# A hybrid decoder layer on one core: the first four weight chunks loaded and split by pairs of k tiles, norm1's gains in a DMA of their own, two DMAs on ScalarE's queue

## The chip, the core and the metric

The kernel runs on one core of a Trainium2 chip. The time is that of one execution on the device, in microseconds. The kernel before took 441.95 us (median of 3 runs, 441.61 to 442.01).

## What is computed

One layer of a decoder trunk with two token mixers side by side and a gated feed-forward network, for 256 tokens of width 1024 in float32:

```python
h = rmsnorm(x, norm1_g)
u = h @ w_in                         # 1024 -> 7168: rnn_x, rnn_gate, q, k, v, two branch gates
A = gelu(rnn_gate) * rg_lru(causal_dwconv4(rnn_x))
B = attention(q, k, v)               # 8 heads of 128, causal, q and k normalised
y = sigmoid(g_A) * (A @ w_proj_rnn) + sigmoid(g_B) * (B @ w_proj_attn)
x = x + y @ w_out
h = rmsnorm(x, norm2_g)
x = x + (gelu(causal_dwconv3(h @ w_up)) * (h @ w_gate)) @ w_down
```

## The kernel before

**Products in three parts.** Every weight and every activation is split into two numbers of TensorE's fast float32 form: `hi` (a rounding copy of `raw`) and `lo` (`raw - hi`). A product is three matmuls, `hi*hi`, `hi*lo` and `lo*hi` (`mm3`, L301 to L304). So for each chunk of weights there is one copy, mostly on ScalarE (L284), one subtraction on VectorE (L285), and 24 or 48 matmuls on TensorE.

**Chunks.** The weights stream through the core in 75 chunks of 1 MB (128 partitions by 2048 numbers; a few are smaller), in the order of `UNITS` (L35) and of the feed-forward part. SyncE's queue loads them, up to three ahead of the one being split (`advance`, L287; `AHEAD_L`). Three buffers hold `raw`, four `hi`, three `lo`. `AFTER` (L37) is a table written out by hand: after such a quarter of such a unit's matmuls, these splits (`s5` is the split of chunk 5) and these other steps stand next in program order. The order within each engine is settled from it when the kernel is built.

**The start.** The first unit, `rx`, is the projection to `rnn_x`: four chunks (0 to 3, 256 columns each, the columns of one chunk at one k tile of 128 rows being 256 numbers of a partition) for eight k tiles. The tiles of x transposed, `xT`, are scaled by norm1's gains into `xgh` (ScalarE, L382) and `xgl` (VectorE, L385); the gains are eight columns of the parameter table `vec` (128 by 170), which is one DMA, `pv` (L324), on ScalarE's queue. All four chunks come in pieces, `pieces` (L333): k tile 0, k tile 1, then k tiles 2-3, 4-5, 6-7; each piece of each chunk has a DMA of its own, 128 KB for one k tile and 256 KB for two (L343 to L347). For the first two pieces, those of chunks 2 and 3 are issued on ScalarE's queue, four DMAs, between which stands the loading of an activation table (L349). The DMAs share eight completion semaphores, and the second two of these four wait on ScalarE's queue until the DMA before them on their semaphore has landed. The split of the pieces (L378 to L387) follows the same order, k tile by k tile; the very first copy is on VectorE. TensorE multiplies nine blocks of ones first (L328 to L330, `warm`), and then takes k tile after k tile, for each the four chunks (`run_unit`, L660 to L667): per chunk and k tile two column halves of three matmuls, six of 128x256, and 192 in all.

**What comes next.** The token sums of norm1 (`norm1_stats`, L393) need `xs`, x by rows, which is loaded between the pieces of k tiles 4-5 and 6-7. They are sent to all partitions by two matmuls with ones (`norm1_bcast`, L402, `rbcp`), copied to `rbc`, and scale the results (`rx_evac`, L437). Then come the `rg` chunks (4 to 7), and the rest of the layer.

## Time and profile before

| | |
|---|---|
| median of 3 runs | 441.95 us (441.61 to 442.01) |
| the profiled execution | 442.97 us, its span 441.2 us |
| TensorE (PE) busy | 435.9 us, 99% of the span |
| VectorE (DVE), ScalarE (ACT) busy | 323.9 us, 260.6 us |
| moved by DMA | 91.68 MB |

The profile is of one execution. PE is TensorE's matmuls, PEld its weight loads, DVE VectorE, ACT ScalarE, SPq and ACTq the queues on which SyncE and ScalarE issue DMAs. Times in the views are microseconds from the span's start; the rows of a timeline are merged where like instructions follow each other (`x3`), the second column is then the length of all of them together, and what stands in brackets is the idle time before and what ended it. The span's start and end leave 1.8 us of the execution's time outside.

### The profile page before, as it was taken

What the parts mean: (1) busy time and instruction counts of PE and PEld (TensorE: products, weight loads), DVE (VectorE), ACT (ScalarE), POOL (GpSimd) and SP (SyncE); (2) the same over time, 40 slices, a digit from 0 to 9 for tenths busy, and PEclk for the clock granted to TensorE, in tenths of its full rate; (3) what the DMA queues carried; (4) which work ended last, traced back from release to release, by engine and by line L of the source; (5) the groups of instructions that cost most, each with busy time, mean ns of one, the idle gap of its engine ahead of it and who ended that gap; (6) DMA issues with size and microseconds to landing.
All of it is one profiled execution on the core that took longest, in us unless ns stands there. A gap on an engine that the chain in (4) does not pass through costs nothing.

```text
span 441.2 us, 5822 instructions
## 1 busy us (share of the span) xinstructions
PE 435.9 (99%) x2256; PEld 373.2 (85%) x2256; DVE 323.9 (73%) x477; ACT 260.6 (59%) x309; POOL 1.6 (0%) x9
## 2 busy tenths in 40 slices
PE   8999999999999999999999999999999999999996
PEld 8999988887888888888888888888878888888985
DVE  3688995979999775754576796468789775788463
ACT  4686875999996989752322384315737554455420
POOL 1000000000000000000000000000000000000000
PEclk9999999999999999999999999999999999999999
DMA  7996536453584653454553554989579598289302
GB/s 209 386 345 236 191 111 249 173 209 102 187 255 123 192 193 114 171 192 179 194 190 104 192 190 133 318 230 326 174 260 348 193 343 345 90 309 351 110 0 95
DMA packets 27387, 91.68 MB, mean 208 GB/s; under 512 B 2528, under 2 KB 10080, under 8 KB 23264
## 3 DMA queue, kind: packets, MB, share of 16 engines
q1 hardware_dynamic: 26640, 90.71, 60.3%
q10 hardware_dynamic: 720, 0.61, 0.6%
q8 instruction: 17, 0.28, 0.2%
q14 instruction: 10, 0.08, 0.1%
HBM read 85.02 MB, written 6.29 MB: 207 GB/s over the span
## 4 chain that ended last, share of the span: by engine, by line
PE 93%; ACT 5%; DMA 1%; issue 0%; DVE 0%; SPq 0%; ACTq 0%
PE acc L303 4%; PE acc L304 4%; PE acc L302 4%; PE up L304 4%; PE up L302 4%; PE gt L302 4%; PE gt L304 4%; PE gt L303 4%; PE up L303 4%; PE rx L302 2%; PE rx L303 2%; PE rx L304 2%; PE rg L303 2%; PE rg L302 2%; PE rg L304 2%; PE gb L302 2%
## 5 line engine op out<-in xcount | busy, mean ns | idle before, releaser
L285 DVE TENSOR_TENSOR lo<-raw,hi 128x2048 fp32r<-128x2048 f32 (+3 forms) x92 | 170.6, 1866 | 29.6 <-issue 11.4
L284 ACT CAST hi<-raw 128x2048 fp32r<-128x2048 f32 (+3 forms) x88 | 137.5, 1577 | 66.6 <-PE pa L304 16.1
L303 PE MATMUL acc<-lo,fah 128*128 128x512 f32 x80 | 31.2, 391 | 0.0
L303 PE MATMUL gt<-lo,h2h 128*128 128x512 f32 x80 | 31.2, 390 | 0.0
L303 PE MATMUL up<-lo,h2h 128*128 128x512 f32 x80 | 31.2, 390 | 0.0
L304 PE MATMUL up<-hi,h2l 128*128 128x512 f32 x80 | 31.1, 389 | 0.0
L304 PE MATMUL acc<-hi,fal 128*128 128x512 f32 x80 | 31.1, 389 | 0.0
L302 PE MATMUL up<-hi,h2h 128*128 128x512 f32 x80 | 31.1, 390 | 0.0
L304 PE MATMUL gt<-hi,h2l 128*128 128x512 f32 x80 | 31.0, 389 | 0.0
L302 PE MATMUL acc<-hi,fah 128*128 128x512 f32 x80 | 30.6, 389 | 0.0
L302 PE MATMUL gt<-hi,h2h 128*128 128x512 f32 x80 | 30.5, 389 | 0.0
L302 PE MATMUL rx<-xgh,hi 128*128 128x256 f32 x64 | 18.9, 298 | 0.7 <-ACT xgh L382 0.7
L303 PE MATMUL rx<-xgl,hi 128*128 128x256 f32 x64 | 18.8, 293 | 0.0
L304 PE MATMUL rx<-xgh,lo 128*128 128x256 f32 x64 | 18.8, 293 | 0.0
L829 ACT ACTIVATE fc<-fu,pv 128x256 f32<-128x256 f32 x20 | 10.4, 592 | 13.7 <-DVE fu L841 13.7
L302 PE MATMUL rg<-xgh,hi 128*128 128x256 f32 x64 | 18.2, 284 | 0.0
L303 PE MATMUL rg<-xgl,hi 128*128 128x256 f32 x64 | 18.1, 283 | 0.0
L304 PE MATMUL rg<-xgh,lo 128*128 128x256 f32 x64 | 18.1, 283 | 0.0
L303 PEld LDWEIGHTS acc<-lo,fah 128*128 128x128 f32 x80 | 15.0, 188 | 3.5 <-DVE lo L285 0.5
L302 PEld LDWEIGHTS gt<-hi,h2h 128*128 128x128 f32 x80 | 15.0, 188 | 3.2
L304 PEld LDWEIGHTS up<-hi,h2l 128*128 128x128 f32 x80 | 15.0, 188 | 3.1
L304 PEld LDWEIGHTS acc<-hi,fal 128*128 128x128 f32 x80 | 15.0, 188 | 3.1
(247 smaller groups left out, 1061.3 us busy)
## 6 DMA issues: line engine op xcount, KB each, us to landing
raw<-in_win_tm SPq DMA_DIRECT2D x12, 1024.0 KB, 4.8
raw<-in_win_fm SPq DMA_DIRECT2D x11, 1024.0 KB, 5.7
raw<-in_wup SPq DMA_DIRECT2D x11, 1024.0 KB, 6.0
raw<-in_wgate SPq DMA_DIRECT2D x11, 1024.0 KB, 6.5
raw<-in_wdown SPq DMA_DIRECT2D x11, 1024.0 KB, 6.4
raw<-in_wpr SPq DMA_DIRECT2D x4, 1024.0 KB, 4.9
raw<-in_wpa SPq DMA_DIRECT2D x4, 1024.0 KB, 4.9
raw<-in_wout SPq DMA_DIRECT2D x4, 1024.0 KB, 4.8
```

Source lines behind the costliest of these rows:

```text
L284: (nc.vector.tensor_copy if on_dve else nc.scalar.copy)(hi[i][:, s], raw[i][:, s])
L285: nc.vector.tensor_sub(lo[i][:, s], raw[i][:, s], f(hi[i][:, s]))
L302: nc.tensor.matmul(o, ah, bh, start=start, stop=False, skip_group_check=skip)
L303: nc.tensor.matmul(o, ah, bl, start=False, stop=False, skip_group_check=skip)
L304: nc.tensor.matmul(o, al, bh, start=False, stop=stop, skip_group_check=skip)
L829: nc.scalar.activation(c, u, AF.Identity, scale=w(2), bias=pv[:, V_FB + m:V_FB + m + 1])
```

## The change

Three edits at the start, and a table of order to go with them.

- **Gains first.** `g1`, a tile of 128 by 8, gets norm1's columns of `vec` in a DMA of its own, the first on ScalarE's queue (32 bytes of each partition). The whole table `pv` is loaded later, on SyncE's queue behind the chunks' pieces.
- **Pieces.** The four chunks are loaded by pairs of k tiles (a = 0 to 3) and pairs of chunks (c = 0, 1), eight pieces of 512 KB; a piece is a tile of 128 by 1024, `sraw`, with rows of 2 KB. The first, (0, 0), is two DMAs of 256 KB: chunk 0 on ScalarE's queue, chunk 1 on SyncE's. Everything else is on SyncE's queue, so that ScalarE issues two DMAs, `g1` and this one. `xs` comes behind all pieces.
- **Splits and products.** The first piece is split in quarters (chunk, k tile) of 128x256, the other seven each in one copy and one subtraction of 128x1024. TensorE takes pairs of k tiles, for each the four chunks: twelve matmuls of one chunk on end, 24 of a piece.
- **Order.** `AFTER` is written anew for the whole layer; two edges (`issue_after`) keep what stands after `rx0` behind the last split of the start.

The core of the diff, with the table of order cut to a few lines:

```diff
-    "rg0.1": "bcast",
-    "rg0.2": "s5 evac1",
-    "rg0.3": "s6",
-    "rg1.1": "evac0",
-    "rg1.3": "evac3 conv0 s7",
+    "rg0.2": "bcast evac1",
+    "rg1.1": "s5 evac0",
+    "rg1.2": "conv0 conv1",
...
-    pv = const.tile([P, V_N], F32, name="pv")
-    nc.scalar.dma_start(pv, vec)
+    g1 = const.tile([P, KT], F32, name="g1")
+    nc.scalar.dma_start(g1, vec[:, V_G1:V_G1 + KT])
...
+    def load_x(a, b):
         nc.sync.dma_start(kt(xTs.half(a // 4))[:, a % 4:a % 4 + b - a, :], xT[:, a:b, :])
-        for i in range(START):
-            s = slice(a * 256, b * 256)
-            (nc.scalar if b <= 2 and i >= 2 else nc.sync).dma_start(raw[i][:, s], stream[i][:, s])
-        if a == 0:
-            nc.scalar.preload_act_table(AF.Exp)
-        if a == 4:
-            for t in range(2):
-                nc.sync.dma_start(xs[:, t, :], x[t * P:(t + 1) * P, :])
+
+    def load_w(q, a, c, js=slice(0, 2)):
+        q.dma_start(sraw[a, c][:, js].rearrange("p c k n -> p c (k n)"),
+                    win_fm[2 * c + js.start:2 * c + js.stop, :, a * 512:(a + 1) * 512].rearrange("c p n -> p c n"))
+
+    load_x(0, 1)
+    load_w(nc.scalar, 0, 0, slice(0, 1))
+    nc.scalar.preload_act_table(AF.Exp)
+    load_w(nc.sync, 0, 0, slice(1, 2))
+    load_x(1, 2)
+    load_w(nc.sync, 0, 1)
+    for a in range(1, 4):
+        load_x(2 * a, 2 * a + 2)
+        for c in range(2):
+            load_w(nc.sync, a, c)
+    pv = const.tile([P, V_N], F32, name="pv")
+    nc.sync.dma_start(pv, vec)
+    for t in range(2):
+        nc.sync.dma_start(xs[:, t, :], x[t * P:(t + 1) * P, :])
...
+        def split_x(k):
+            g = g1[:, k:k + 1]
+            nc.scalar.activation(xgh[k], xTs[k], AF.Copy, scale=g)
+            return lambda: nc.vector.scalar_tensor_tensor(xgl[k], xTs[k], g, f(xgh[k]), op0=OP.mult, op1=OP.subtract)
+
+        def split_w(a, c, js=slice(0, 2), ks=slice(0, 2), e=nc.scalar.copy):
+            r, h, l = sraw[a, c][:, js, ks], shi[a, c][:, js, ks], slo[a, c][:, js, ks]
+            start_end[0] = e(h, r).ins
+            return lambda: start_end.__setitem__(1, nc.vector.tensor_sub(l, r, f(h)).ins)
+
+        one, two_ = slice(0, 1), slice(1, 2)
+        x0 = split_x(0)
+        w0 = split_w(0, 0, one, one, nc.vector.tensor_copy)
+        x0()
+        w0()
+        w1 = split_w(0, 0, two_, one)
+        w1()
+        w0 = split_w(0, 0, one, two_)
+        x1 = split_x(1)
+        x1()
+        w0()
+        split_w(0, 0, two_, two_)()
+        split_w(0, 1)()
+        for a in range(1, 4):
+            for k in (2 * a, 2 * a + 1):
+                split_x(k)()
+            for c in range(2):
+                split_w(a, c)()
...
-            for k in range(KT):
+            for a in range(KT // 2):
                 for n in range(START):
-                    fm_mm(rx_ps[n], n, xgh, xgl, (k,), True)
+                    fm_mm(rx_ps[n], n, xgh, xgl, (2 * a, 2 * a + 1), True)
```

More of the change, by code (lines that the diff above doesn't have):

```diff
@@ L1 @@
-from contextlib import ExitStack
+from contextlib import ExitStack, nullcontext
 import concourse.bass as bass
@@ L38 @@
     "rx0.0": "stats s4",
-    "rg0.1": "bcast",
-    "rg0.2": "s5 evac1",
-    "rg0.3": "s6",
-    "rg1.1": "evac0",
-    "rg1.3": "evac3 conv0 s7",
+    "rg0.2": "bcast evac1",
+    "rg1.1": "s5 evac0",
+    "rg1.2": "conv0 conv1",
     "rg2.0": "evac2",
-    "rg2.1": "decay conv1",
+    "rg2.1": "decay",
+    "rg2.2": "s6",
+    "rg2.3": "s7",
     "rg3.0": "split0",
     "rg3.1": "s8",
+    "rg3.2": "evac3",
     "k0.0": "s9",
@@ L50 @@
     "k0.2": "conv3",
-    "k0.3": "split1",
     "k1.0": "s10",
-    "k1.3": "s11",
+    "k1.2": "s11",
     "k2.1": "s12",
-    "k2.2": "s13",
-    "k3.1": "s14 gelu1",
-    "ri0.2": "krs",
-    "ri0.3": "s15",
+    "k2.2": "split1 s13",
+    "k3.2": "gelu1",
+    "k3.3": "s14",
+    "ri0.1": "s15",
     "q0.1": "la0 s16 lb0",
     "q1.1": "s17",
-    "q1.3": "lc0",
-    "ri1.0": "s18",
-    "q2.0": "ld0",
-    "q2.1": "s19",
-    "q2.2": "la1",
-    "q3.0": "lb1 Tq0",
+    "q1.2": "krs",
+    "q2.2": "s18 la1",
+    "q2.3": "s19 lc0",
+    "q3.0": "Tq0",
     "q3.1": "ks0",
     "q3.2": "gelu0",
+    "q3.3": "lb1",
     "v0.1": "qrs",
     "v0.3": "s20 Tk0",
-    "v1.1": "s21",
+    "v1.2": "ld0",
+    "v1.3": "s21",
     "v2.1": "S0 s22",
-    "v3.0": "ks1",
-    "v3.1": "Tk1",
-    "v3.2": "s23",
+    "v2.3": "ks1",
+    "v3.2": "s23 Tk1",
     "v3.3": "lc1 S1 S2",
-    "ga0.2": "s24 P0",
+    "ga0.0": "P0",
+    "ga0.2": "s24",
     "ga1.0": "S3",
-    "ga1.1": "s25 P1 O0",
+    "ga1.1": "s25",
+    "ga1.2": "P1 Tq1",
     "ga1.3": "s26",
-    "ga2.0": "Tq1",
-    "ga2.1": "P2",
+    "ga2.0": "P2",
+    "ga2.1": "O0",
     "ga2.3": "s27",
-    "ga3.1": "P3",
-    "ga3.2": "O1 S5 S6",
-    "ga3.3": "S7 O3",
-    "gb0.1": "S4",
-    "gb0.3": "s28",
-    "gb1.0": "O2",
-    "gb1.2": "ld1 s29",
-    "gb1.3": "P4",
-    "gb2.0": "s30 s31",
-    "gb2.1": "P6 ya0 ya1 O4",
-    "gb2.3": "P5",
-    "gb3.0": "P7",
-    "gb3.1": "ys0",
+    "ga3.0": "P3",
+    "ga3.1": "S5",
+    "ga3.2": "O1 S6",
+    "ga3.3": "O3",
+    "gb0.0": "O2 S4",
+    "gb0.2": "S7 s28",
+    "gb1.0": "ld1",
+    "gb1.3": "s29 P4",
+    "gb2.0": "ya1 s30",
+    "gb2.1": "P6 s31 O4",
+    "gb2.2": "s32",
+    "gb2.3": "P5 P7",
+    "gb3.1": "sb0 ya0 ys0",
     "gb3.3": "ys1",
-    "pr0.0": "s32 sb0",
+    "pr0.0": "s33",
     "pr0.2": "sa0",
-    "pr0.3": "s33",
-    "pr1.0": "O7",
+    "pr0.3": "O7",
     "pr1.2": "s34",
-    "pr2.0": "sa1 O6",
-    "pr2.2": "O5",
+    "pr2.0": "sa1",
+    "pr3.2": "O5",
     "pr3.3": "sb1",
-    "pa0.0": "s35 s36",
+    "pa0.0": "s35 O6 s36",
     "pa0.3": "s37",
@@ L109 @@
     "pa2.1": "s39",
-    "pa2.2": "s40 m0",
+    "pa2.2": "m0",
     "pa3.3": "m1",
-    "wo.3": "s41",
-    "wo.4": "m2",
-    "wo.6": "m3",
+    "wo.0": "s40",
+    "wo.6": "m2",
+    "wo.7": "s41 m3",
     "wo.11": "n10 s42",
     "wo.12": "n00",
-    "wo.14": "s43",
+    "wo.13": "s43",
     "up00.0": "n01 s44",
-    "up00.1": "n11",
+    "up00.1": "n11 s45",
     "up00.3": "bcast2",
-    "gt00.0": "s45",
     "up01.0": "s46",
-    "gt01.0": "s47",
-    "gt01.1": "ur0",
-    "up10.1": "s48",
-    "up10.2": "gr0",
-    "up11.1": "s49",
-    "up11.3": "fu0",
+    "gt01.1": "s47",
+    "gt01.3": "ur0",
+    "up10.2": "s48 s49",
+    "up11.2": "gr0",
     "gt10.1": "s50",
-    "gt10.2": "ur1",
+    "gt10.2": "fu0 ur1",
     "gt11.1": "s51 fg0",
     "up20.1": "s52",
-    "up20.2": "gr1",
-    "up20.3": "fu1",
+    "up20.2": "fu1",
+    "up21.0": "gr1",
     "up21.1": "s53",
     "gt20.1": "s54",
-    "gt20.2": "ur2",
-    "gt20.3": "fg1",
-    "gt21.1": "s55",
+    "gt21.0": "ur2 fg1 s55",
     "dn0.1": "s56",
     "dn0.2": "gr2",
-    "dn0.3": "fu2",
     "dn1.1": "s57",
     "up30.1": "s58",
-    "up30.3": "fg2",
-    "up31.1": "s59",
-    "gt30.1": "s60",
-    "gt30.2": "ur3",
-    "gt31.1": "s61",
-    "dn2.1": "s62",
+    "up30.2": "fu2",
+    "up31.3": "s59",
+    "gt30.1": "fg2 s60 s61",
+    "gt31.1": "s62",
+    "dn2.0": "ur3",
     "dn2.2": "gr3",
@@ L153 @@
     "dn3.1": "s63",
-    "up40.1": "s64",
-    "up40.3": "fg3",
-    "up41.1": "s65",
-    "gt40.1": "s66",
+    "up40.1": "s64 s65",
+    "gt40.1": "fg3 s66",
     "gt40.2": "ur4",
-    "gt41.1": "s67",
-    "dn4.1": "s68",
+    "gt41.0": "fu4",
+    "gt41.2": "s67",
     "dn4.2": "gr4",
-    "dn4.3": "fu4",
-    "dn5.1": "s69",
+    "dn4.3": "s68",
+    "dn5.0": "s69",
     "dn6.1": "s70",
-    "dn6.3": "fg4",
-    "dn7.1": "s71",
-    "last.0": "s72",
+    "dn6.2": "fg4",
+    "dn7.3": "s71",
+    "last.1": "s72",
     "last.2": "s73",
-    "dn8.1": "s74",
+    "dn9.3": "s74",
 }
@@ L213, in pair, with __init__ @@
             return kt(self.half(c // 2))[:, 2 * (c % 2):2 * (c % 2) + 2, :]
-    class Wide:
-        def __init__(self, name, dt=F32):
-            self.h = [half(f"{name}{i}", dt) for i in range(2)]
+    class Column:
+        def __init__(self, pieces, i):
+            self.pieces, self.i = pieces, i
         def __getitem__(self, at):
-            s = at[1]
-            i = s.start // 1024
-            assert (s.stop - 1) // 1024 == i
-            return self.h[i][:, s.start - i * 1024:s.stop - i * 1024]
+            k, c = divmod(at[1].start, 256)
+            return self.pieces[k // 2, self.i // 2][:, self.i % 2, k % 2, c:c + at[1].stop - at[1].start]
     stream = []
@@ L330, in trunk_layer, with pieces @@
         nc.tensor.matmul(warm[:, :P], ones, ones, start=True, stop=True)
-    pieces = [(0, 1), (1, 2), (2, 4), (4, 6), (6, 8)]
     START = 4
-    for i in range(START):
-        if i < 2:
-            raw[i] = wp.tile([P, 2048], F32, tag="raw", name=f"raw{i}")
-            split_tiles()
-        else:
-            raw[i], hi[i], lo[i] = Wide(f"raw{i}"), Wide(f"hi{i}", F32R), Wide(f"lo{i}", F32R)
+    def pieces(name, dt=F32):
+        p = {}
+        for a in range(2):
+            t = wp.tile([P, 2048], dt, tag=name, name=f"{name}s{a}", bufs={"raw": RAWS, "hi": 4, "lo": 3}[name])
+            for c in range(2):
+                p[a, c], p[a + 2, c] = t[:, c * 1024:(c + 1) * 1024], half(f"{name}s{a + 2}{c}", dt)
+        return {k: v.rearrange("p (c k n) -> p c k n", c=2, k=2) for k, v in p.items()}
+    sraw, shi, slo = pieces("raw"), pieces("hi", F32R), pieces("lo", F32R)
+    for i in range(START):
+        hi[i], lo[i] = Column(shi, i), Column(slo, i)
     ptr["load"] = ptr["split"] = START
     xs = const.tile([P, 2, D], F32, name="xs")
-    for a, b in pieces:
+    def load_x(a, b):
         nc.sync.dma_start(kt(xTs.half(a // 4))[:, a % 4:a % 4 + b - a, :], xT[:, a:b, :])
-        for i in range(START):
-            s = slice(a * 256, b * 256)
-            (nc.scalar if b <= 2 and i >= 2 else nc.sync).dma_start(raw[i][:, s], stream[i][:, s])
-        if a == 0:
-            nc.scalar.preload_act_table(AF.Exp)
-        if a == 4:
-            for t in range(2):
-                nc.sync.dma_start(xs[:, t, :], x[t * P:(t + 1) * P, :])
+    def load_w(q, a, c, js=slice(0, 2)):
[15 more added lines that the diff above has]
+        nc.sync.dma_start(xs[:, t, :], x[t * P:(t + 1) * P, :])
     load_next(2)
@@ L378, in trunk_layer @@
     with tc.manual_schedule(engines={mybir.EngineType.Activation, mybir.EngineType.DVE}):
-        for a, b in pieces:
-            for k in range(a, b):
-                g = pv[:, V_G1 + k:V_G1 + k + 1]
-                nc.scalar.activation(xgh[k], xTs[k], AF.Copy, scale=g)
-                if a == 0:
-                    split_part(0, slice(a * 256, b * 256), True)
-                nc.vector.scalar_tensor_tensor(xgl[k], xTs[k], g, f(xgh[k]), op0=OP.mult, op1=OP.subtract)
-            for i in range(a == 0, START):
-                split_part(i, slice(a * 256, b * 256))
+        start_end = [None, None]
+        def split_x(k):
[22 more added lines that the diff above has]
+                split_x(k)()
+            for c in range(2):
+                split_w(a, c)()
     rbc = const.tile([P, S], F32, name="rbc")
@@ L715, in run @@
         for q, _ in enumerate(quarters):
-            for n in AFTER.get(f"{name}.{q}", "").split():
-                advance(int(n[1:])) if n[1:].isdigit() and n[0] == "s" else item[n]()
+            with tc.issue_after(start_end[0]) if name == "rx0" else nullcontext(), \
+                    tc.issue_after(start_end[1]) if name == "rx0" else nullcontext():
+                for n in AFTER.get(f"{name}.{q}", "").split():
+                    advance(int(n[1:])) if n[1:].isdigit() and n[0] == "s" else item[n]()
     yo = {}
```

## The prediction

> **What bounds the kernel now.** I read the page's first lines, then who waits on TensorE, then the start instruction by instruction. The page:

> ```profile
> span 441.2 us, 5822 instructions
> PE 435.9 (99%) x2256; PEld 373.2 (85%) x2256; DVE 323.9 (73%) x477; ACT 260.6 (59%) x309; POOL 1.6 (0%) x9
> ```

> Whom TensorE's matmuls waited for in the whole span (us in total, times, longest):

> ```profile
> PE warm L330 <- DVE ones L326: 1.1, 1, 1.1
> PE rx L302 <- ACT xgh L382: 0.7, 1, 0.7
> ```

> These are all of its waits, and both lie ahead of the first real matmul. From there on TensorE is never without work for long enough to be listed. A gain from this change must therefore come from the first real matmul's start, or from the pace of TensorE behind it. Its timeline there:

> ```profile
> 4.20 1.06 PE L330 MATMUL warm<-ones 128*128 128x128 f32 x4
> 5.94 0.88 PE L302 MATMUL rx<-xgh,hi 128*128 128x256 f32 x2 [0.68 <-ACT xgh L382]
> 6.61 0.43 PE L303 MATMUL rx<-xgl,hi 128*128 128x256 f32 x1
> ...
> 9.19 0.41 PE L304 MATMUL rx<-xgh,lo 128*128 128x256 f32 x1
> 9.40 0.33 PE L302 MATMUL rx<-xgh,hi 128*128 128x256 f32 x1
> 9.57 0.28 PE L303 MATMUL rx<-xgl,hi 128*128 128x256 f32 x1
> 9.69 0.28 PE L304 MATMUL rx<-xgh,lo 128*128 128x256 f32 x1
> ```

> The starts are 0.21 us apart up to 9.40, and 0.12 from 9.57 on: the clock of TensorE doubles at about 9.5. (The clock shows only in this spacing; the page's own clock line reads 9 from the first slice.) Sixteen matmuls start from 5.94 to 9.40, so 9.5 us have bought sixteen of the unit's 192 (three lines of the page like this one, x64 each):

> ```profile
> L302 PE MATMUL rx<-xgh,hi 128*128 128x256 f32 x64 | 18.9, 298 | 0.7 <-ACT xgh L382 0.7
> ```

> Why 5.94? The chain of waits of the first 8 us:

> ```profile
> 0.74 0.38 SPq L344
> 1.18 3.80 DMA raw<-in_win_fm
> 5.00 0.33 ACTq L347
> 5.38 0.52 ACT xgh L382
> 5.94 0.88 PE rx L302 x2
> ```

> A chunk piece lands at 4.97; that lets ScalarE issue its last queued DMA (5.00 to 5.33), and only then can it compute `xgh`. Yet the inputs of `xgh` were there before: `xT`'s first tile, issued at 0.74, took 3.6 us (the shortest of `xT`'s five DMAs, to 4.34), `pv`, issued beside it, 3.8 (to 4.54):

> ```profile
> DMA to landing us min/median/max: 3.6/5.2/7.6
> pv<-in_vec ACTq DMA_DIRECT2D x1, 85.0 KB, 3.8
> ```

> **The change, part by part.**

> *Two DMAs on ScalarE's queue, and the small `g1`.* The rows of ScalarE and of VectorE about the first matmul; the first of them goes, the others give the durations used below:

> ```profile
> 4.36 0.97 ACTq L347 DMA_DIRECT2D raw<-in_win_fm  x2
> 5.38 0.51 ACT L382 ACTIVATE xgh<-xT,pv 128x256 fp32r<-128x256 f32 x1 [1.96 <-DMA raw<-in_win_fm]
> 5.79 1.00 ACT L284 CAST hi<-raw 128x256 fp32r<-128x256 f32 x3
> 5.00 0.29 DVE L284 CAST hi<-raw 128x256 fp32r<-128x256 f32 x1 [4.00 <-DMA raw<-in_win_fm]
> 5.92 0.48 DVE L385 SCALAR_TENSOR_TENSOR xgl<-xT,pv,xgh 128x256 fp32r<-128x256 f32 x1 [0.17 <-ACT xgh L382]
> 6.32 1.08 DVE L285 TENSOR_TENSOR lo<-raw,hi 128x256 fp32r<-128x256 f32 x3
> ```

> The 0.97 us of issuing leave ScalarE, so `xgh` can run from 4.34 and end at about 4.9, well ahead of the first piece. The stall moves: late next is the piece itself, then VectorE's copy of it (0.29). Had the piece still landed at 4.97, the first matmul would start at 4.97 + 0.03 + 0.29 + 0.05 = 5.34, 0.6 us sooner. `g1` has 32 bytes of each partition; no row shows such short ones, but it decides nothing as long as it lands before 4.9, and `pv`, twenty times its bytes in as many rows, was there at 4.54. [...]

> *Pieces of 256 and 512 KB.* They take back most of that. In the kernel before, 128 KB each of `xT`, chunk 0 and chunk 1 (SyncE) and 85 + 128 + part of 128 KB (ScalarE) are under way together, and the third of SyncE's lands 4.0 us after its issue at about 1.63, at 5.65:

> ```profile
> 1.18 0.89 SPq L347 DMA_DIRECT2D raw<-in_win_fm  x2
> raw<-in_win_fm SPq DMA_DIRECT2D x1, 128.0 KB, 4.0
> 4.00:5.00 1.00, 1.00 (x6) 0.96 (x5) 0.00 (x1) 0.00 (x0) 0.00 (x0) 1.00 1.07 364
> 12.00:13.00 1.00, 1.00 (x10) 1.00 (x10) 1.00 (x2) 0.94 (x2) 0.00 (x0) 1.00 1.07 410
> ```

> By then 597 to 725 KB have landed. The changed kernel needs 128 + 4 + 256 + 256 = 644 KB for its first piece, since both halves run at once and share the rate. At the old pace that is about 5.6; the rows of 2 KB move faster than those of 1 KB (the last two of the rows above are of stretches of 1 us, with GB/s in the last column: 410 against 364), so I take 5.5, between 4.97 and 5.65 and nearer the second. The first matmul starts at 5.5 + 0.37 = 5.87: a gain of 0.07 in place of 0.6.

> *The next matmuls.* With 0.33 us for a copy and 0.51 for an `xgh` on ScalarE, 0.36 for a subtraction and 0.48 for an `xgl` on VectorE (the rows above; of three on end the third part), in the order of the changed kernel: VectorE has `xgl` of k tile 0 at 6.3, `lo` of chunk 0 at 6.65, of chunk 1 at 7.0. `xT`'s second tile, 128 KB more, lands at 5.85; `xgh` of k tile 1 is third behind two copies on ScalarE and done at 6.7, its `xgl` at 7.5, the `lo` of chunk 0 at 7.85. TensorE starts its matmuls at 5.87, 6.08, 6.3, 6.7, 6.9, 7.1, 7.5, 7.7 and 7.9, and then nothing is late: the 15 left of the piece go 0.21 apart. By 9.5 it has begun 16 or 17, against 16 before. Early starts are worth only half, as they lie in the slow stretch: one matmul is 0.12 us. I take **-0.1 us**; with the piece at 4.97 it would be 19, -0.36; with 5.65, 0 to +0.1.

> *The other seven pieces.* Each costs ScalarE and VectorE one instruction in place of several:

> ```profile
> L284 ACT CAST hi<-raw 128x1024 fp32r<-128x1024 f32 x2 | 2.1, 1032 | 0.0
> L285 DVE TENSOR_TENSOR lo<-raw,hi 128x1024 fp32r<-128x1024 f32 x2 | 2.5, 1226 | 1.3 <-ACT hi L284 1.3
> ```

> Piece (0, 1) lands 1.3 us behind `xT`'s second tile, at 7.15, is copied by 8.2 and subtracted by 9.4. TensorE asks for it with its 27th matmul, at 9.5 + 10 x 0.12 = 10.7. Cover: 1.3 us. From there a piece feeds TensorE for 24 x 0.12 = 2.9 us, while DMA needs 1.3 (512 KB at 400 GB/s) or 1.6 with `xT`'s share, VectorE 1.23 + 0.48; the cover grows with each piece. Without it, each late tenth is a tenth of the end. The hole in the transfers about 8 us goes too, but TensorE waited for none of it: nothing.

> *`pv` and `xs` behind the pieces, `dg` behind two subtractions.* VectorE's `dg`, which the `rbcp` matmul needs, now stands behind the subtractions of chunks 5 and 6. Before:

> ```profile
> 30.63 0.48 DVE L400 TENSOR_SCALAR dg<-ident,rs 128x128 f32<-128x128 f32 x2
> 31.03 4.49 DVE L285 TENSOR_TENSOR lo<-raw,hi 128x2048 fp32r<-128x2048 f32 x2
> 33.55 0.60 PE L406 MATMUL rbcp<-dg,ones 128*128 128x128 f32 x4
> ```

> Left where they are, the two would put `dg` at 30.6 + 4.5 + 0.5 = 35.6, and TensorE asks at 33.55 + 12 x 0.12 = 35.0 (`bcast` moves back by one quarter): 0.6 us lost. But their loads no longer wait for buffers held to the end of the start; 9.5 MB up to chunk 6, of which 0.65 have landed at 5.5, end at 400 GB/s at about 28, copy and subtraction at 32, `dg` at 32.5. Cover 2.5 us, cost nothing. `pv` is first used behind `rbc`.

> *The rest of the order.* The same matmuls, one activation table load fewer, other places. What the old order loses shows in the weight loads' waits, of which those behind the start are 1.8 us in all, most of it hidden by the matmul under way:

> ```profile
> PEld Tq L546 <- ACT it L463: 0.5, 1, 0.5
> PEld acc L303 <- DVE lo L285: 0.5, 1, 0.5
> PEld h2T L746 <- DVE xs L739: 0.3, 1, 0.3
> PEld rbfp L794 <- DVE dg L791: 0.3, 1, 0.3
> PEld yo L304 <- DVE ml L299: 0.2, 1, 0.2
> ```

> So between -0.9 (half of what is listed) and, if one subtraction of 2.2 us comes late by its own length, +2. I take 0, as nothing in the new order puts one next to its use that I could find.

> **Sum.** 442.97 (the profiled execution: span 441.2 and 1.8 around it) - 0.1 = 442.87. The median of the runs is 1.0 below the profiled one: 441.95 - 0.1, or **441.8 us**.

> **The rivals.**

> 1. *The clock rises one stretch sooner.* TensorE ran ones from 1.05 to 5.26, stood until 5.94, and doubled its pace 3.5 us later. If the pause is what put this off, a first matmul at 5.3 might close it, and the pace double 3.5 us sooner, at about 6.0. Then VectorE sets the pace to the ninth matmul at 7.8, fifteen follow by 9.6: 25 begun by 9.5 in place of 16, 9 x 0.12 = -1.1 us, and -1.4 with the earlier start, so 440.7. For it: the start that follows the pause by 3.5 us. Against: my first matmul comes at 5.87, and 4.2 us of ones alone were not enough. [...]
> 2. *Slower: the clock rises one stretch later.* The place is the first nine matmuls, the price a further 3.5 us at half pace: 16 matmuls for 29, 13 x 0.12 = +1.5 us, 443.4. Before, two matmuls of 0.21 fill 0.43 of the 0.67 us from 5.94 to 6.61; these 0.24 us of pause did not hinder the clock, while the 0.68 ahead of them may have. My pauses are 0.2 ahead of the fourth and 0.2 ahead of the seventh; it decides once pieces and `xT` land so late that they pass some 0.6.
> 3. *A split of the new order comes late* (after 60 us), up to +2: 442.5 to 443.9.
> 4. *The change does not bring the start forward at all*, since the first piece lands at 5.65 or later: +0.1, 442.0. This falls in the forecast's own bounds.

> **How the numbers follow.** Forecast and rival 4: 0.62, 441.4 to 442.3. Rival 1: 0.15. Gains of the new order beyond the terms: 0.05. Rival 2: 0.09. Rival 3: 0.09. A measurement of this kernel can tell about 0.2%, 0.9 us, from no change. Faster by more: rival 1 and the gains, 0.20. Slower: rivals 2 and 3, 0.18. The same: 0.62. The range goes to rival 1 with the earliest landing, 440.4, and takes in half of rival 3, to 442.9; rival 2 and the rest of 3 stay out (about 0.15).

> **What would show it.** Right: ScalarE's `xgh` ahead of 5.0; the first `rx` matmul at 5.8 to 5.9, waiting for VectorE's copy and that for its DMA at 5.5; spacing 0.12 from about 9.5; no wait on TensorE from 8 us on; `rg` begun within 0.2 us of where it was. Wrong: a first matmul at 5.3, a doubled pace at another time than 9.5, or a wait in the later stages.

## The result, and the profile after

The changed kernel took **443.16 us** (median of 15 runs, 442.86 to 443.39), the kernel before, in runs of the same measurement, 442.54 us (441.50 to 443.19). The ratio is 1.0017, with a 95% interval of 1.0010 to 1.0025: slower, by little, and above the forecast's range. Measured again later beside the experiments, it was 443.30 us against 441.79, 1.0031 (1.0022 to 1.0040). The two kernels also differ in their scatter: 1.7 us for the kernel before, 0.5 for the changed one.

The page and the whole list of TensorE's matmul waits of the profile after (this execution took 442.86 us, as little as the fastest of the fifteen):

```profile
span 441.1 us, 5781 instructions
PE 435.5 (99%) x2256; PEld 373.4 (85%) x2256; DVE 323.7 (73%) x468; ACT 258.1 (59%) x299; POOL 1.5 (0%) x9
```

```profile
PE warm L319 <- DVE ones L315: 1.1, 1, 1.1
PE rx L291 <- DVE his L395: 1.0, 1, 1.0
```

TensorE still stands only ahead of the first real matmul, now 1.0 us in place of 0.7, and for VectorE's copy in place of ScalarE's `xgh`. The chain of waits of the start (start, length, what):

```profile
0.73 0.41 ACTq L313
1.14 0.03 issue
1.17 4.58 DMA raws<-in_win_fm
5.76 0.02 issue
5.78 0.30 DVE his L395
6.09 0.14 issue
6.22 0.77 PE rx L291 x2
```

The first piece of 256 KB lands at 5.76 (forecast 5.5); the first matmul starts at 6.22 (forecast 5.87). `xgh` had long been done, and the pace doubles at 10.03 in place of 9.50 (timelines of ScalarE and of TensorE):

```profile
3.47 0.51 ACT L390 ACTIVATE xgh<-xT,g 128x256 fp32r<-128x256 f32 x1 [0.53 <-DMA g<-in_vec]
```

```profile
9.68 0.41 PE L291 MATMUL rx<-xgh,his 128*128 128x256 f32 x1
9.89 0.35 PE L292 MATMUL rx<-xgl,his 128*128 128x256 f32 x1
10.08 0.28 PE L293 MATMUL rx<-xgh,los 128*128 128x256 f32 x1
10.20 0.28 PE L291 MATMUL rx<-xgh,his 128*128 128x256 f32 x1
```

By unit, the profiled execution after stands against the one before as follows: the last `rx` matmul 0.40 us later, the last of `q` 0.06 later, the last matmul of all 0.23 sooner. Two waits that the old order had, ahead of `Tq` and of `acc`, are gone (0.34 and 0.33 us). So this pair of profiles says -0.1 us, as forecast, while fifteen runs of each say +0.6. The pair misleads, and the experiments had to show which of the two profiles is not like its runs.

### The profile page after: what moved, and what is told of

Same layout as the page of the kernel before. It is cut to its first block, busy times and chain, and to the rows that moved or that the text cites. A ratio compares the mean times of both kernels' runs of the same rounds, so it can differ in the third digit from the quotient of the medians.

```text
span 441.1 us, 5781 instructions
## 1 busy us (share of the span) xinstructions
PE 435.5 (99%) x2256; PEld 373.4 (85%) x2256; DVE 323.7 (73%) x468; ACT 258.1 (59%) x299; POOL 1.5 (0%) x9
## 4 chain that ended last, share of the span: by engine, by line
PE 98%; DMA 1%; DVE 0%; ACTq 0%; issue 0%
PE acc L293 4%; PE acc L291 4%; PE acc L292 4%; PE up L293 4%; PE gt L293 4%; PE gt L291 4%; PE up L291 4%; PE gt L292 4%; PE up L292 4%; PE rx L291 2%; PE rx L292 2%; PE rx L293 2%; PE rg L293 2%; PE rg L292 2%; PE rg L291 2%; PE gb L291 2%
## 5 line engine op out<-in xcount | busy, mean ns | idle before, releaser
L274 DVE TENSOR_TENSOR lo<-raw,hi 128x2048 fp32r<-128x2048 f32 (+1 forms) x72 | 160.2, 2225 | 41.7 <-ACT hi L273 6.4
L273 ACT CAST hi<-raw 128x2048 fp32r<-128x2048 f32 (+1 forms) x69 | 128.2, 1863 | 68.9 <-PE pa L293 13.0
L291 PE MATMUL rx<-xgh,his 128*128 128x256 f32 x64 | 18.8, 297 | 1.0 <-DVE his L395 1.0
L292 PE MATMUL rx<-xgl,his 128*128 128x256 f32 x64 | 18.7, 296 | 0.0
L293 PE MATMUL rx<-xgh,los 128*128 128x256 f32 x64 | 18.6, 294 | 0.0
L292 PEld LDWEIGHTS gt<-lo,h2h 128*128 128x128 f32 x80 | 15.0, 188 | 3.1
L293 PEld LDWEIGHTS gt<-hi,h2l 128*128 128x128 f32 x80 | 15.0, 188 | 3.1
```

The source lines that it names most:

```text
L273: (nc.vector.tensor_copy if on_dve else nc.scalar.copy)(hi[i][:, s], raw[i][:, s])
L274: nc.vector.tensor_sub(lo[i][:, s], raw[i][:, s], f(hi[i][:, s]))
L291: nc.tensor.matmul(o, ah, bh, start=start, stop=False, skip_group_check=skip)
L292: nc.tensor.matmul(o, ah, bl, start=False, stop=False, skip_group_check=skip)
L293: nc.tensor.matmul(o, al, bh, start=False, stop=stop, skip_group_check=skip)
```

## The experiments

Three theories at first. **A**: the start costs a constant, since the first piece lands later. **B**, sharpened to **D**: the clock decides; by this theory it changes only at the edges of windows of 3.41 us (the profile after has it full for 430.079 us, 126 times 3.413), and what precedes an edge settles it. **C**: the new order costs. Later came **E** and **G** (the size of the transfers), **F** (their rate about 8 us), **H** (the wide copies and subtractions), **I** (the order by pairs) and **J** (two limits, one behind the other). All times are medians; "before" is the kernel before, measured among the same runs.

| run | us | before | ratio (95%) |
|---|---|---|---|
| e1_start_only | 444.51 | 441.93 | 1.0058 (1.0045 to 1.0071) |
| e2_order_only | 441.40 | 441.93 | 0.9992 (0.9978 to 1.0006) |
| e3_small_two_dmas | 442.20 | 441.93 | 1.0013 (1.0001 to 1.0025) |
| e4_before_again | 442.01 | 441.93 | 1.0003 (0.9992 to 1.0014) |
| e5_after_warm12 | 443.13 | 441.70 | 1.0035 (1.0023 to 1.0046) |
| e6_before_warm6 | 442.56 | 441.70 | 1.0016 (1.0006 to 1.0025) |
| e7_before_warm12 | 442.02 | 441.70 | 1.0012 (0.9999 to 1.0025) |
| e8_after_small_first | 443.54 | 441.70 | 1.0037 (1.0023 to 1.0052) |
| e9_after_small_both | 443.73 | 441.79 | 1.0048 (1.0029 to 1.0067) |
| e10_small_start_new_order | 441.86 | 441.79 | 1.0004 (0.9989 to 1.0019) |
| e11_order_only_again | 441.36 | 441.79 | 0.9993 (0.9979 to 1.0007) |
| e12_after_again | 443.30 | 441.79 | 1.0031 (1.0022 to 1.0040) |
| e13_after_old_dma_sizes | 443.82 | 441.91 | 1.0059 (1.0035 to 1.0082) |
| e14_after_old_sizes | 444.19 | 441.91 | 1.0063 (1.0043 to 1.0084) |
| e15_after_old_first_two | 446.25 | 441.91 | 1.0092 (1.0072 to 1.0112) |
| e16_after_old_sizes_dg_first | 441.74 | 441.68 | 0.9998 (0.9986 to 1.0011) |
| e17_after_dg_first | 443.12 | 441.68 | 1.0030 (1.0019 to 1.0040) |

**Which part costs: start, order, or the DMA split?** e1 is the changed kernel with the old table `AFTER`; e2 the kernel before with the new table; e3 the kernel before with

```diff
-    nc.scalar.dma_start(pv, vec)
+    nc.scalar.dma_start(g1, vec[:, V_G1:V_G1 + KT])
...
-            (nc.scalar if b <= 2 and i >= 2 else nc.sync).dma_start(raw[i][:, s], stream[i][:, s])
+            (nc.scalar if a == 0 and i >= 2 else nc.sync).dma_start(raw[i][:, s], stream[i][:, s])
```

and `pv` ahead of `xs`; e4 the kernel before, unchanged.

> The changed kernel's start (pieces by pairs, g1, two DMAs on ScalarE) with the old table AFTER. Theory A (the start costs a constant: in the two profiles its rx unit ends 0.40 us later, first matmul 6.22 for 5.94): 0.35 to 0.45 us over the kernel before, with the same scatter from run to run (1.7 us). Theory B (the scatter of the kernel before comes from where the free-running clock window of 3.41 us falls, and coarse pieces cannot use an early edge): 443.0 to 443.2 us, 0.5 to 0.7 over the kernel before, and a scatter of about 0.5 us as the changed kernel has. Theory C (the new order costs, not the start): within 0.2 us of the kernel before.

> The old start with the new table AFTER. Theory A: the two late weight loads of the profile before (0.34 us ahead of q's end, 0.33 ahead of acc) go, so 0.4 to 0.7 us under the kernel before. Theory B: as A or no difference, and a scatter as wide as the kernel before's (about 1.7 us). Theory C: 0.6 to 1.0 us over the kernel before, with a scatter of 0.5 us.

> The kernel before with its small pieces and its old order, but g1 ahead of pv and only the first k tile of chunks 2 and 3 on ScalarE's queue. By the prediction's own second step xgh ends by 4.9 and the first matmul follows VectorE's copy at 5.34. Theory A: 0.3 us under the kernel before (0.6 earlier, half of it kept at half pace), first matmul 5.3 to 5.5. Theory B: the same on the mean, scatter 1.7 us. If the queue of SyncE, now with two more transfers of 128 KB, delays the second k tile, the gain goes: within 0.1 us.

> The kernel before once more, unchanged, so that the granted clock of each of its runs is on record beside its time. All theories: ratio 1.000 within 0.001. Theory B: the time rises with the place of the clock's edge, up to 1.7 us from the fastest to the slowest run; theories A and C: time and clock not related.

C falls: the start alone costs 2.6 us, more than any theory gave it, and the new order by itself gains about 0.5 (e2, and again e11), an interval that just includes no change. The two DMAs with `g1` gain nothing; e3 is 0.3 us slower, if anything. The profile of e4 (441.36 us, the second fastest of its twelve runs) tells why, and why the forecast's ground was bad. Its TensorE and VectorE:

```profile
2.92 2.22 PE L330 MATMUL warm<-ones 128*128 128x128 f32 x10
4.95 0.91 PE L302 MATMUL rx<-xgh,hi 128*128 128x256 f32 x2
5.70 0.28 PE L303 MATMUL rx<-xgl,hi 128*128 128x256 f32 x1
5.82 0.28 PE L304 MATMUL rx<-xgh,lo 128*128 128x256 f32 x1
```

```profile
4.01 0.29 DVE L284 CAST hi<-raw 128x256 fp32r<-128x256 f32 x1 [3.01 <-DMA raw<-in_win_fm]
```

Here the first piece is there at 3.99, not 4.97; the first real matmul follows the ones at 4.95 with no pause (no bracket), and the spacing is 0.12 from the third on. The records of the clock have it full from 4.88. The profile of the kernel before on which the forecast stands is an execution whose first transfers came 1 us later, with a pause of 0.7 us, and a clock that rose at 9.50: it took 442.97 us, longer than 13 of the 15 runs of its own measurement. Between the two, the last `rx` matmul differs by 1.56 us (30.55 and 28.99), and the two executions' times by 1.61. In e2 and e11, whose start is the same, the clock rises at 6.19 and 4.86, so the early rise is the more common one as far as four profiles tell. The runs of e4 can't test theory B: their granted clock counts the time ahead of the first rise as full, and is 0.999 or 1.000 in all twelve.

In e1 the clock rose early, at 4.56, and was taken away again. Stretches of 1 us, the third column from the right is the granted clock:

```profile
7.00:8.00 1.00, 0.89 (x6) 0.65 (x6) 1.00 (x4) 0.00 (x0) 0.00 (x0) 0.99 0.77 193
8.00:9.00 1.00, 1.00 (x6) 1.00 (x6) 0.07 (x1) 0.00 (x0) 0.00 (x0) 0.50 0.97 336
11.00:12.00 1.00, 0.81 (x6) 0.61 (x4) 1.00 (x2) 0.54 (x3) 0.00 (x0) 0.81 1.03 399
```

Half pace from 7.97 to 11.38, one window: that is the price of the prediction's second rival, though there the clock was to rise late, and here it rose and fell again. And `rbcp` waits for `dg` here, 0.5 us on the weight load's side; the prediction had 0.6 for this wait, and only if the loads stayed where they were.

**The pause by itself.** e5 is the changed kernel, e6 and e7 the kernel before, with another number of matmuls of ones (9 in both):

```diff
-HALVES, SMALLS, WARM, RAWS = 22, 10, 9, 3
+HALVES, SMALLS, WARM, RAWS = 22, 10, 12, 3     (e6: 6)
```

> The changed kernel with 12 matmuls of ones in place of 9, so that TensorE does not stand between them and the first real matmul at 6.1 to 6.2. Theory D (the pause of about 1 us, which the 256 KB pieces leave, costs the clock a window of 3.41 us, and so 1 to 1.7 us; in a usual run of the kernel before the pause is missing): no window at half pace behind 7.9 us in the records of the clock, first matmul 6.2 to 6.7, and 0.5 to 0.9 us under the changed kernel, 442.3 to 442.7 (not less: piece (0, 1) is subtracted only at 10.2, and TensorE then waits for it). Theory A (only the landing of the first pieces costs): 443.1 to 443.6, since three more ones can only put the first matmul back.

> The kernel before with 6 matmuls of ones in place of 9: they end near 3.9 us, and TensorE stands for about 1 us until the first real matmul at 4.9 to 5.1, with all transfers as before. Theory D: the clock is not at full pace before 8 us, or loses a window behind it; 0.8 to 1.6 us over the kernel before, 442.8 to 443.6, so that the pause alone does what the change did. Theory A: no difference from the kernel before within 0.3 us, since pieces and first matmul are where they were.

> The kernel before with 12 matmuls of ones: the control. Theory D: it had no pause to bridge in a usual run, so the three more ones only put the first real matmul back, from 4.95 to between 5.6 and 6.7 by the place of the clock's edge: 0.1 to 0.6 us over the kernel before, scatter smaller than 1.7 us. If more ones were good in themselves: 0.3 us or more under it.

e6 comes out as D says, if a little under its 442.8 to 443.6 us: the transfers are where they were, TensorE stands 1.00 us, the clock stays down until 8.38, and the kernel before loses 0.86 us. e7, the control, loses 0.3, an interval that just includes no change. TensorE of e6:

```profile
4.99 1.07 PE L302 MATMUL rx<-xgh,hi 128*128 128x256 f32 x2 [1.00 <-ACT xgh L382]
...
8.20 0.37 PE L303 MATMUL rx<-xgl,hi 128*128 128x256 f32 x1
8.41 0.28 PE L304 MATMUL rx<-xgh,lo 128*128 128x256 f32 x1
```

But e5 fails D. Its clock is full from 4.64 and stays so, as expected, and it is as slow as the changed kernel (443.13 us; theory A had 443.1 to 443.6). The clock is not all of it. Behind the ones its TensorE waits 0.6 us for the first copy, and 0.8 for the subtraction of piece (0, 1):

```profile
PE rx L293 <- DVE los L396: 0.8, 1, 0.8
PE rx L291 <- DVE his L395: 0.6, 1, 0.6
```

The same shows in the changed kernel's second profile (e12): the clock is up from 5.75, without the late edge or the lost window that D expected, and the execution took 443.54 us, longer than the first with its edge at 10.03 (442.86). Its chain of waits says what stands in the way:

```profile
2.10 7.19 DMA raws<-in_win_fm
9.29 0.02 issue
9.31 1.06 ACT his L395
10.38 0.02 issue
10.40 1.24 DVE los L396
11.64 0.04 issue
11.68 0.39 PE rx L293
```

Piece (0, 1), 512 KB, lands at 9.29; then 1.06 us of copy and 1.24 of subtraction pass before TensorE goes on at 11.68. With a slow clock TensorE asks for it later and hardly notices; with a fast one it waits. The first profile after can't show this alone, as its piece also landed sooner, at 7.83. But in e17 below, the changed kernel with one edit, the piece lands at 9.12, the clock rises at 9.90, and TensorE waits 0.3 us. In all three the `rx` unit ends at about the same time (30.95, 31.58 and 31.39). That would explain the narrow scatter: the kernel before turns an early clock into time, the changed kernel can't; it is argued from these profiles.

The granted clocks of all runs say the same. Six of the changed kernel's first fifteen and five of its twelve in e12 have a granted clock of 0.996. The 0.004 that are missing are about 1.7 us of 441, half of 3.41: by this estimate these runs lost one window after the first rise. None of the 116 runs of the kernel before beside the experiments is below 0.998. Yet the runs with a lost window are only 0.1 (first fifteen) and 0.3 us (e12) slower than the others, by their medians.

> The changed kernel again, beside these on one chip. Theories D and E: 1.0 to 1.6 us over the kernel before, all of it by the end of the rx unit; the clock's edge later than 8.5 us, or a window at half pace behind an early one; piece (0, 1) landed between 7.8 and 9.5.

**Is it the size of the first transfers?** In e8 the first piece is four transfers of 128 KB by k tile; e9 also cuts piece (0, 1) into two of 256 KB, each with its own copy and subtraction.

```diff
-    load_w(nc.scalar, 0, 0, slice(0, 1))
+    load_w(nc.scalar, 0, 0, slice(0, 1), 0, 1)     # chunk 0, k tile 0
...
-    load_w(nc.sync, 0, 1)
+    for c in range(2):                              # e9 only
+        load_w(nc.sync, 0, 1, slice(c, c + 1))
```

> The changed kernel with the first piece (chunks 0 and 1, k tiles 0 and 1) in four transfers of 128 KB by k tile in place of two of 256 KB; everything behind it as changed. Theory D: first piece lands at about 4.1, first matmul 4.9 to 5.3 right behind the ones, clock at full pace by 6.5 and kept; rx still ends late, as piece (0, 1) of 512 KB is subtracted only at about 10: 442.2 to 442.7. Theory A: the landing alone, 0.5 to 0.6 us, of which half is kept at half pace: 442.8 to 442.9 and the clock as it falls.

> The changed kernel with the first piece in four transfers of 128 KB by k tile, as in the run before, and piece (0, 1) in two of 256 KB, each copied and subtracted by itself. Theory D with E (D: a pause ahead of or within the first matmuls costs the clock a window; E: the 512 KB of piece (0, 1), landed at 9.0 to 9.5 in these runs, leave TensorE standing once it runs at full pace from 5 us): the two stops of 1.5 and 0.8 us shrink to under 1 us together, no window at half pace behind 8 us, and the time falls by 1.0 to 1.8 us against the run with only the first piece small: 441.8 to 442.5 where the kernel before is at 441.8. If the transfers' rate about 8 us sets the landing and not their size (theory F): the second half lands at 9.0 to 9.5 as before, the stops stay over 1.5 us, and the time falls by less than 0.5 us.

Both start at 4.91, without a pause, and neither is any faster; e8, at 443.54, lies above what D (442.2 to 442.7) and A (442.8 to 442.9) gave it, so the late first piece by itself is not what costs, and A falls. The gain at the start is given back at piece (0, 1): behind the ones, TensorE's waits in e8 are

```profile
PE rx L291 <- ACT his L397: 1.5, 1, 1.5
PE rx L293 <- DVE los L398: 0.8, 1, 0.8
```

and in e9 1.2 and 0.8; E falls, as far as two halves go. In e9 they landed at 7.80 and 9.53, so F has something: between 7 and 8 us the transfers slow down, whatever the kernel. After, and e4:

```profile
7.00:8.00 1.00, 1.00 (x6) 0.98 (x6) 1.00 (x4) 0.15 (x1) 0.00 (x0) 1.00 0.76 215
```

```profile
7.00:8.00 1.00, 1.00 (x11) 1.00 (x10) 0.77 (x3) 0.71 (x2) 0.00 (x0) 1.00 0.76 218
```

215 and 218 GB/s, against 414 in the stretch from 9 of the profile after. The kernel before meets this stretch too (its last 128 KB of k tile 1 land at 9.10 in e4), but it has 42 matmuls, 5.0 us at 0.12 each, to do ahead of that piece; the changed kernel has 24 ahead of piece (0, 1).

**Order alone on the small start.** e10 is e3 with the new table, e11 repeats e2.

> The old start's small pieces with g1 first and two transfers less on ScalarE's queue, and the new table AFTER: two of the three parts of the change, without the large pieces. Theories D and E: rx as in the run with these two DMAs and the old order (first matmul 4.9, clock up by 6.5), then the new order's 0.6 us: 0.3 to 0.6 us under the kernel before. If the new order pays only behind the coarse start: no difference from the kernel before within 0.2 us.

> The old start and the new table AFTER once more, for a narrower interval. Theories D and E: 0.4 to 0.7 us under the kernel before, the version that beats both.

e11 confirms e2 (441.36 us); e10 does not reach it, and its runs spread from 441.1 to 444.0, so whether the order pays on that start stays open.

**Transfers, copies, or order by pairs?** e13 puts the old sizes of all transfers into the changed kernel; e14 the sizes of copies and subtractions too; e15 the old first two k tiles, with the large pieces behind them.

```diff
+    def load_w(q, a, c, js=slice(0, 2), k=0, n=2):  # e13 to e15: by chunk and k tile
...
-        split_w(0, 1)()                             # e14: 256 columns, 512 for a >= 1
+        for j in (one, two_):
+            for k in (one, two_):
+                split_w(0, 1, j, k)()
...
-            for a in range(KT // 2):                # e15
+            for ks in ((0,), (1,), (2, 3), (4, 5), (6, 7)):
```

> The changed kernel with its transfers as small as before (128 KB by chunk and k tile for the first two k tiles, 256 KB by chunk behind them); copies, subtractions and TensorE's order by pairs as changed. Theory G (the size of the transfers: a piece is there only when the slowest of its parts is): within 0.4 us of the kernel before, 441.4 to 442.2. Theory H (the wide copies and subtractions, 1.03 and 1.23 us for 1024 columns) and theory I (the order by pairs): 443.0 us or more, as the changed kernel.

> The run before, with the copies and subtractions small too: 256 columns in the first two k tiles, 512 behind them. What is left of the change is g1, two DMAs on ScalarE, TensorE's order by pairs, pv behind the pieces, and the table. Theory H: 441.2 to 442.0, where the run with only the transfers small stays at 443. Theory G: as that run. Theory I: still 443.0 or more, since with the order by pairs TensorE asks for chunk 2 after 24 matmuls, at 8 us at full pace, in the stretch from 7 to 9.5 us in which the transfers of all profiles are slow.

> The changed kernel with its first two k tiles as in the kernel before (128 KB transfers, copies of 256 columns, all four chunks of a k tile before the next), and the 512 KB pieces from k tile 2 on. Theories G, H and I alike put the loss into the first two k tiles, if TensorE has 48 matmuls, 5.8 us at full pace, from what has landed by 7 to 9.5 us: 441.3 to 442.0, at or under the kernel before. If the large pieces behind cost as well: 442.5 or more, with a wait for a copy or subtraction of k tile 2 at 11 to 13 us.

None came out as a time, and the three profiles together give most of the answer. TensorE's waits behind the ones, of e13, of e14 and of e15:

```profile
PE rx L291 <- ACT his L400: 1.9, 1, 1.9
PE rx L293 <- DVE los L401: 0.8, 1, 0.8
```

```profile
PE rbcp L442 <- DVE dg L436: 1.7, 1, 1.7
PE rx L293 <- DVE los L401: 0.2, 1, 0.2
PE rx L291 <- ACT his L400: 0.2, 1, 0.2
```

```profile
PE rx L291 <- ACT his L398: 2.6, 1, 2.6
PE rx L293 <- DVE los L399: 0.8, 1, 0.8
```

Small transfers alone do nothing (G falls): the wide copy still waits for the last of the four, landed at 9.39. With small copies too, the waits in `rx` shrink from 2.7 us to 0.4 and `rx` ends at 30.17, 1.4 us before e12's, although the last of the four transfers lands later still, at 10.19; that is H, as far as `rx` goes. (Small copies on large transfers were not run, so whether they need the small transfers is open.) I falls with it, since e14 keeps the order by pairs. e15 shows the same at the next place: with the first two k tiles cut small, TensorE runs into the first large piece behind them and stands 3.4 us, and the clock is lost for a window from 16.4.

And e14 is no faster, since it waits 1.7 us for `dg`, a second limit. VectorE in the changed kernel's first profile:

```profile
29.84 2.29 DVE L274 TENSOR_TENSOR lo<-raw,hi 128x2048 fp32r<-128x2048 f32 x1
32.05 0.15 DVE L381 SCALAR_TENSOR_TENSOR rs<-rsq 128x2 f32<-128x2 f32 x1
32.12 2.29 DVE L274 TENSOR_TENSOR lo<-raw,hi 128x2048 fp32r<-128x2048 f32 x1
34.32 0.48 DVE L428 TENSOR_SCALAR dg<-ident,rs 128x128 f32<-128x128 f32 x2
```

and TensorE there:

```profile
35.38 0.61 PE L434 MATMUL rbcp<-dg,ones 128*128 128x128 f32 x4
```

`dg` is done at 34.8, 0.6 us ahead of its use (0.7 in e12), and an `rx` unit that ends more than that sooner gains nothing by it. In e14 this limit has moved as well: `dg` is done at 36.6. It stands behind the subtractions of chunks 4 to 6, and the first of these begins 1.8 us later than in the changed kernel (the profile after, then e14; 26.15 in e16):

```profile
24.62 1.23 DVE L274 TENSOR_TENSOR lo<-raw,hi 128x1024 fp32r<-128x1024 f32 x1 [3.68 <-ACT hi L273]
26.45 1.23 DVE L274 TENSOR_TENSOR lo<-raw,hi 128x1024 fp32r<-128x1024 f32 x1 [3.80 <-ACT hi L273]
```

The loads fall behind with the small transfers: 209 and 340 GB/s from 8 to 9 and from 9 to 10 us, against 379 and 414. So small transfers have a price of their own, which e14 pays at `dg`; why they move less is open.

**Both limits taken away.** In e16 and e17 the subtractions of chunks 5 and 6 are put behind `dg` on VectorE; e16 on top of e14, e17 in the changed kernel:

```diff
-        nc.vector.tensor_sub(lo[i][:, s], raw[i][:, s], f(hi[i][:, s]))
+        with tc.issue_after(dg_done[-1]) if i in (5, 6) else nullcontext():
+            nc.vector.tensor_sub(lo[i][:, s], raw[i][:, s], f(hi[i][:, s]))
```

> The version with small transfers and small copies and subtractions, and VectorE's subtractions of chunks 5 and 6 put behind dg. Theory J (two limits behind one another: the wide pieces of the start, then dg's place): TensorE's wait for dg, 1.7 us, goes; 441.6 to 442.4, as the kernel before within 0.5 us. If a third limit stands behind: over 443.

> The changed kernel with the subtractions of chunks 5 and 6 behind dg and nothing else. Theory J: in its two profiles TensorE reached rbcp 0.7 to 0.8 us behind dg, so the start alone is the limit there: no difference from the changed kernel within 0.3 us, 443.0 to 443.5, with faster runs at most where the start is early. If dg's place is what holds all of the changed kernel's runs near 443.2: 442.6 or less.

Both as J has it. e17 is as slow as the changed kernel, e16 as fast as the kernel before, and its waits behind the ones are

```profile
PE rx L294 <- DVE los L402: 0.2, 1, 0.2
PE rx L292 <- ACT his L401: 0.2, 1, 0.2
```

Against e17, which has the wide pieces, it gains 1.4 us; against e14, which has `dg` late, 2.2 us (e14 is 2.28 over the kernel before of its measurement, e16 0.06), of which the profiles show 2.1 at the last matmul: 2.0 within `rg`, where that wait stood, and 0.2 in `rx`. The fastest version is still the old start with the new table, 441.4 us.

## Why the prediction was wrong, by its own steps

- **What bounds the kernel (wrong for the other executions seen).** "16 matmuls begun by 9.5" and "early starts are worth only half" hold for the one execution that was profiled. In e4 the clock is full at the first matmul, 4.95 us, in e2 and e11 from 6.19 and 4.86, so there each tenth of the start is a whole tenth, or nearly. The sign was on the page: the prediction found the profiled execution 1.0 us above the median and carried this through the sum as a constant, when it lay in the very stretch that the change edits.
- **`xgh` freed from ScalarE's DMAs (right, and worth nothing).** It ends at 3.98; `g1`, with its rows of 32 bytes, had landed at 3.44. But TensorE is busy with its ones until 4.9, and e3 gains nothing.
- **The first piece (mechanism right, size off).** It landed at 5.76, not 5.5; the rows of 2 KB were no faster there, 309 and 334 GB/s from 4 to 6 us against 364 and 307 in the profile before. Against e4 the first matmul is 1.27 us later (6.22), in e12 1.49 (6.44). The prediction had -0.1 us for this term. The pause it opens is what the second rival describes; put into the kernel before, a pause of 1.00 us costs 0.86 us (e6). In the changed kernel itself this term is not what costs: e8 and e9 start at 4.91 and gain nothing.
- **The other pieces: "cover 1.3 us, growing" (wrong; this step decides).** Forecast for piece (0, 1): landed 7.15, copied 8.2, subtracted 9.4. Measured: landed 7.83 in the first profile after, 9.29 in the second (9.52 in e1, 8.99 in e5, 9.12 in e17), subtracted 10.15 in the first and 11.6 in the second. In the first the cover held, 1.0 us, with the clock up only at 10.03; in the second TensorE was ready for the 27th matmul 0.8 us before the subtraction let it begin. The working had the piece 1.3 us behind `xT`'s second tile, at 400 GB/s; it came 1.7 and 3.1 us behind it, and from 7 to 8 us only 215 and 238 GB/s are moved there. "The hole in the transfers about 8 us goes too" did not hold: it is in every profile. And TensorE's demand was held at half pace. One copy and one subtraction "in place of several" was counted as a saving; on the path they are 2.3 us behind the last byte, where two narrow ones would be 0.8 by estimate (0.39 and 0.42 us each).
- **`dg` behind two subtractions (size wrong, cost right).** Forecast 32.5, measured 34.8, so the cover is 0.6 us and not 2.5. It costs nothing in the changed kernel as it stands (e17), and 1.7 us in e14, where the start is mended and the loads come 1.8 us later.
- **The rest of the order (undersized).** Taken as 0 with -0.9 as a bound; the two waits it named are gone, 0.67 us in the profiles and about 0.45 alone (e2, e11). It hides part of the start's loss: between e4 and e12, `rx` ends 2.6 us later, the last matmul 2.1.
- **The rivals.** The second had a window at half pace, which 11 of 27 runs of the changed kernel lost, and 0.09; but the clock alone would not have made the changed kernel slow, as e5 and e12 show. None had the late second piece. The 3.5 us of the first two was the distance from the first matmul to the rise in one profile; in the runs the rise lies from 1.6 us ahead of the first matmul (e5) to 3.8 behind it (the profile after), and the lost stretch of e1 is 3.41. The fourth (start not brought forward) is what the first term came to, at 1.3 us in place of 0.1.

In sum, against e4's execution: first matmul 1.3 to 1.5 us later; the rest of the 2.0 to 2.6 by which `rx` ends later is either half pace up to 10.0 (first profile) or waiting for piece (0, 1) (second); less 0.5 to 0.6 by the order. That gives 1.4 to 2.1, where the two measurements have 0.6 and 1.5 of medians. Part of the difference is that e4's execution is a fast one, 0.65 us below the median of its twelve runs. Why the first measurement has so much less than the second is open: its runs of the kernel before were slower (442.54 against 441.7 to 441.9 in all later ones), as if more of them began like the profiled one.

## What to carry to other kernels

Before costing a change to a kernel's first microseconds, compare the profiled execution with the spread of the runs: a difference of 1 us between them may be a different start, and then the terms worked out there hold for that start alone. A larger piece saves instructions in sum and adds its whole transfer, copy and subtraction ahead of the first use (in e12 7.19, 1.06 and 1.24 us for piece (0, 1)); at the start of this kernel, where nothing is in hand yet, the second weighed more. Small transfers are not free either: in e14 chunk 4 came 1.8 us later behind them. When a limit is taken away and nothing is gained, ask the next wait on the list before giving up the theory.

## What the runs showed of the hardware

**The clock's windows.** In the records of the profiles before and after, the clock is full for 433.493 and 430.079 us on end, 127 and 126 times 3.413; the stretches at half pace of e1 (7.97 to 11.38) and e15 (16.4 to 19.8) are 3.4 us long. The first rise lies anywhere from 3.92 (e10) to 10.03 us (after) from the span's start, and 3.92, 4.56 (e1), 4.88 (e4), 5.75 (e12) and 6.19 (e2) are no whole windows apart, so in these traces the windows begin at no fixed place of the span. What went ahead of a rise and of a fall in these traces: TensorE's idle time in the 3.413 us ahead of an edge, an estimate from the starts of its matmuls, the ones included, less 0.12 us (0.21 at half pace) for each:

| idle in the window | what the clock did at its end |
|---|---|
| 0.31 (before), 0.50 (e6), 0.74 (e12), 0.75 (e10) | rose |
| 0.92 (before), 1.02 (e9), 1.24 (e17), 1.34 (after) | stayed down |
| 1.48 (e5), 1.55 (e12), 1.76 (e9), 1.89 (e13), 1.92 (e10) | stayed up |
| 1.94 (e8), 2.07 (e1), 2.19 (e15) | fell for one window |

**The slow stretch of the transfers.** Between 7 and 8 us the transfers move 78 to 238 GB/s in every profile of this case, whatever is loaded and in whatever sizes; from 9 to 10 it is 248 to 414. In e1, eleven of the sixteen parts of piece (0, 1) had landed by 7.35 and the last five between 8.18 and 9.52; its copy begins at 9.54. In the profile after, fifteen had landed by 7.43 and the last at 7.83; its copy begins at 7.85. In both the copy began only behind the last part, 2.2 and 0.4 us behind the eleventh and the fifteenth. What slows the last parts down at this place is open.
